# Neighbourhood attention on tiles of two half blocks: 64 queries with keys of their own, scores in plain fp32

## The chip, the cores and the metric

The kernel runs on one core of a Trainium2 chip. The metric is the device time of one launch in microseconds, the median of several runs. A program's engines are called PE (TensorE), DVE (VectorE), ACT (ScalarE), POOL (GpSimd) and SP (the queue that issues all transfers).

## What is computed

One encoder layer on two sequences, a prompt of 256 and a sample of 2048 tokens, both seen as a grid of 64 columns (4 and 32 rows). Half of the mixing is attention over a window of 8 rows by 16 columns around each query, with a bias by relative place; the other half is a Fourier mixing.

```python
def one_row(r):
    rs = jnp.clip(r - kr // 2, 0, rows - kr)          # kr = min(8, rows)
    k_slab = lax.dynamic_slice_in_dim(kg, rs, kr, axis=1)[:, :, slab_cols]
    v_slab = lax.dynamic_slice_in_dim(vg, rs, kr, axis=1)[:, :, slab_cols]
    logits = jnp.einsum('bjqhd,bijkhd->bhjqik', q_blk, k_slab).astype(jnp.float32) * scale
    logits = jnp.where(valid[:, :, None, :], logits + bias, NEG_INF)
    p = jax.nn.softmax(...)
    out = jnp.einsum('bhjqik,bijkhd->bjqhd', p, v_slab)

h = rms_norm(x, g_pre)
q, k, v, z_a, u_f, z_f = jnp.split(h @ w_in, ...)
mixed = concat([rms_norm(attention(q, k, v)) * silu(z_a), rms_norm(fourier(u_f)) * silu(z_f)])
out = x + rms_norm(mixed @ w_out, g_post)
```

There are 8 heads of 64 features; they are worked on in 4 pairs, one head on partitions 0 to 63 and the other on 64 to 127.

## The kernel before, in words

The program has three parts. First the projections (about 0 to 560 us): large matmuls in which each fp32 operand is split into a high and a low fp32r half, three products for one (`mm3`, L164 to L166). In this part the tables of the attention bias are also masked and written to DRAM (`t_load`, `t_mask`, `t_store`, L578 to L600). Then the Fourier part (to about 625 us), then attention together with the first half of the output projection (to 887 us), then the rest of the output projection.

Attention goes over 36 groups, `G`: for each head pair one group of the prompt (`R` is None) and eight of the sample (`R` 0 to 3 is a block of 8 query rows, `hc` the left or right half of the columns). A group has two query tiles `b` of 128 queries. In the sample a tile is 8 rows by 16 columns. All 128 queries share one rectangle of keys, which covers the windows of all of them: 11, 15, 15 or 12 rows (`NR`, from row `K0` on) by 24 or 32 columns (`KW`), so 264 to 480 keys; in the prompt 4 rows by 40 columns. What a query may not see is masked by the bias table.

For one group: `scores` multiplies q (K = 64, one head) with the keys into four PSUM tiles, a tile for each `b` and head. q and K are split into fp32r halves first (`split_q`, L1137; `split_k`, L1069, a quarter of K at a time, in the groups 5 to 8 of the pair before), by a cast on ACT and a subtraction on POOL, and three matmuls are summed (L1157). The heads' matmuls use rows 0 to 63 and 64 to 127 of the array. `bias_max` on DVE adds the table and takes the extreme (L1179), `exps` on ACT takes the exponential with its sum (L1184), `soft` on POOL scales (L1191). `transp` (L1462) turns the weights in chunks of up to 128 keys on PE into `ptb` and copies them to `pt` (one head by ACT, one by DVE). `pv` multiplies them with V, plain fp32, the heads in two column tiles of the array (L1478), then DVE multiplies by z, ACT squares, POOL sums.

The order on PE, ACT, DVE, POOL and SP is written by hand in the loop over `k`: scores of group `k`; transposes of `b` = 0 of group `k - 1`; six matmuls of the output projection of the Fourier half (`f_mm`, `po`, L1408); transposes of `b` = 1; six more; `pv` of group `k - 1`. So at each moment the vector engines work on group `k` while PE finishes group `k - 1`. K of the next pair is loaded at `i` = 3, the bias tables at `i` = 0, 3 and 7, q three groups ahead (`prep`), V and z one group ahead of the scores (`prep_v`).

Of the kernel before, what the change touches and what calls it, by code (L numbers as in the profile page):

```python
# [29 lines left out]
NR = (11, 15, 15, 12)  # L30
K0 = (0, 4, 12, 20)
KW = (24, 32, 32, 24)
KC0 = (0, 8, 24, 40)
YB = 2
# [9 lines left out]
def constants():  # L44
# [59 lines left out]
    cm = np.zeros((128, 2, 40))  # L104
    cs_ = np.zeros((128, 80))
    rm = np.zeros((128, 48))
    for p in range(128):
        for b in range(2):
            ws = min(max(32 * b + p % 32 - 8, 0), 48)
            kc = 24 * b + np.arange(40)  # L110
            cm[p, b] = np.where((kc >= ws) & (kc < ws + 16), 0.0, BIG)
        i, qc = divmod(p, 16)
# [4 lines left out]
        for r0, j in ((max(i - 4, 0), np.arange(11)), (i, 11 + np.arange(15)), (min(i, 4), 26 + np.arange(12))):  # L117
            rm[p, j] = np.where((j - j[0] >= r0) & (j - j[0] < r0 + 8), 0.0, BIG)
    c["cmask"] = cm.reshape(128, 80)
# [5 lines left out]
def layout(inp):  # L125
# [15 lines left out]
    d = np.arange(40)[None, :] - np.arange(32)[:, None]  # L141
    cols = np.clip(np.stack([d, d - 8]) + 15, 0, 30)
    rows = np.arange(4)[None, :] - np.arange(4)[:, None] + 7
    a["tp"] = rpb[:, rows[:, None, None, :, None], cols[None, :, :, None, :]].reshape(4, 2, 4, 2, 32, 4, 40) \
        .transpose(0, 2, 4, 3, 1, 5, 6).reshape(4, 128, 640)
    d = np.arange(32)[None, :] - np.arange(16)[:, None]
    cols = np.clip(np.concatenate([d[:, :24], d - 8, d[:, :24] - 8], 1) + 15, 0, 30)
    rows = np.clip(np.arange(15)[None, :] - np.arange(8)[:, None] + 3, 0, 14)
    a["tr"] = rpb[:, rows[:, None, :, None], cols[None, :, None, :]].reshape(8, 128, 1200)
# [19 lines left out]
def build(tc, A, O):  # L169
# [10 lines left out]
    vP = dr.tile([2, 4, 40, 512], F32, name="vP")  # L180
# [10 lines left out]
    tD = [dr.tile([4, 128, 2, 80 * n], F32, name="tD%d" % n) for n in (11, 15, 12)]  # L191
# [13 lines left out]
    cm = cst.tile([128, 2, 40], F32, name="cm")  # L205
# [130 lines left out]
    def vu_out(m, c):  # L336
        s, b = PL[c]
        o = st.tile([128, 512], F32, tag="f", name=m + "o", bufs=3)
        x = row_tile(c)
        nc.scalar.activation(o, acc.pop((m, c)), AF.Copy, scale=invt[:, x:x + 1])  # L340
        if s is not None:
            put_rows(m, 0, b, s, o)
        elif m == "u":
            nc.sync.dma_start(uD[c * 128:c * 128 + 128, :], o)
        else:
            for r in range(4):
                nc.sync.dma_start(vP[c, r, 8 * c:8 * c + 32], o[32 * r:32 * r + 32])
                x = 24 * (1 - c)
                nc.sync.dma_start(vP[1 - c, r, 32 * c:32 * c + 8], o[32 * r + x:32 * r + x + 8])
# [228 lines left out]
    def t_load(x):  # L578
        mt.extend(k8(F32, "mt", (128, 2048)) for y in range(2))
        nc.sync.dma_start(mt[0][:, :1200], A["tr"][x])  # L580

    def t_mask(x, q):
        rows = lambda a: a.rearrange("p (i x) -> p i x", x=80)
        base, out = rows(mt[0][:, :1200]), rows(mt[1][:, :1840])
        if q == 0:
            nc.vector.tensor_tensor(out=base, in0=csm.unsqueeze(1).to_broadcast([128, 15, 80]), in1=base,  # L586
                                    op=ALU.subtract)
            return
        o, i, m0, n = ((out[:, :11], base[:, 4:], 0, 11), (out[:, 11:], base[:, :12], 26, 12), (base, base, 11, 15))[q - 1]
        nc.gpsimd.tensor_tensor(out=o, in0=i, in1=rmask[:, m0:m0 + n].unsqueeze(2).to_broadcast([128, n, 80]),  # L590
                                op=ALU.add)

    def t_store(x, q):
        pr, h = divmod(x, 2)
        if q == 0:
            nc.sync.dma_start(tD[0][pr][:, h], mt[1][:, :880])
            nc.sync.dma_start(tD[2][pr][:, h], mt[1][:, 880:1840])
        else:
            nc.sync.dma_start(tD[1][pr][:, h], mt[0][:, :1200])
            mt.clear()  # L600
# [138 lines left out]
    for b in range(16):  # L739
# [25 lines left out]
        if kind % 2:  # L765
            i, d = p, o
        else:
            i = p.rearrange("p (b r c) -> p b r c", b=2, c=32)
            d = o.rearrange("p (r b c) -> p b r c", b=2, c=32)
        nc.scalar.activation(d, i, AF.Silu if kind < 2 else AF.Copy)  # L770
# [8 lines left out]
    def t_step(x, j):  # L779
        if j == 0:  # L780
            t_load(x)
        for q in {3: (0, 1), 4: (2,), 5: (3,)}.get(j, ()):
            t_mask(x, q)
        if j > 4:
            t_store(x, j - 5)
# [30 lines left out]
    for i in range(16):  # L816
# [22 lines left out]
        def dst(f, b):  # L839
            if kind % 2 == 0:  # L840
                return o[f].rearrange("p (x b c) -> p b x c", b=2, c=32)[:, b]
            if kind == 1:
                return o[f].rearrange("p (a b j) -> p b a j", b=2, j=256)[:, b]
            return o[f].rearrange("p (y b x c) -> p y x b c", y=2, b=2, c=16)[:, b]

        def src(a):
            if kind % 2 == 0:
                return a.rearrange("p (x c) -> p x c", c=32)
            if kind == 1:
                return a.rearrange("p (a j) -> p a j", j=256)  # L850
# [207 lines left out]
    KQ = T // 4  # L1058
# [6 lines left out]
    def fetch_k(kk, pr, x):  # L1065
        ts = slice(x * (T // 2), (x + 1) * (T // 2))
        nc.sync.dma_start(kk[1][:, ts].bitcast(F32), kD[pr, :, ts])

    def split_k(kk, x):  # L1069
        ts = slice(x * KQ, (x + 1) * KQ)  # L1070
        nc.scalar.copy(kk[0][:, ts], kk[1][:, ts].bitcast(F32))
        nc.gpsimd.tensor_tensor(out=kk[1][:, ts], in0=kk[1][:, ts].bitcast(F32), in1=kk[0][:, ts].bitcast(F32),
                                op=ALU.subtract)


    TB = {}

    def load_t(pr, kind):
        t = TB[pr, kind] = tp.tile([128, 2400], F32, tag="tb", name="tb", bufs=2)
        if kind == 0:  # L1080
            nc.sync.dma_start(t[:, :640], A["tp"][pr])
            nc.sync.dma_start(t[:, 640:].rearrange("p (h x) -> p h x", h=2), tD[0][pr])
        else:
            n = 80 * (15, 12)[kind - 1]
            nc.sync.dma_start(t[:, :2 * n].rearrange("p (h x) -> p h x", h=2), tD[kind][pr])

    def mask_p(pr):
        v = TB[pr, 0][:, :640].rearrange("p (b x c) -> p b x c", b=2, c=40)
        nc.gpsimd.tensor_tensor(out=v, in0=cm.unsqueeze(2).to_broadcast([128, 2, 8, 40]), in1=v, op=ALU.subtract)
# [3 lines left out]
    def group(pr, i):  # L1093
        if i == 0:
            return dict(pr=pr, R=None, ts=slice(0, TP), k0=0, nr=4, t=[(24 * b, 40) for b in range(2)])
        R, hc = divmod(i - 1, 2)
        t0 = TP + 512 * R + 256 * hc
        return dict(pr=pr, R=R, hc=hc, ts=slice(t0, t0 + 256), k0=4 + K0[R], nr=NR[R],
                    t=[(KC0[2 * hc + b], KW[2 * hc + b]) for b in range(2)])

    def prep(g):
        pr, ts = g["pr"], g["ts"]
        g["qh"] = jl.tile([128, 256], F32R, tag="qh", name="qh", bufs=4)
        g["ql"] = jl.tile([128, 256], F32R, tag="ql", name="ql", bufs=4)
        if g["R"] is None:
            q = qD[pr, :, ts].rearrange("p (b x) -> p b x", b=2)
        else:
            sg, x = divmod(g["R"], 2)
            t0 = TP + 1024 * sg + 512 * g["hc"]
            q = qD[pr, :, t0:t0 + 512].rearrange("p (b x) -> p b x", b=2)[:, :, 128 * x:128 * x + 128]  # L1110
        nc.sync.dma_start(g["ql"].bitcast(F32).rearrange("p (b x) -> p b x", b=2), q)


    def prep_v(g):
        cs = slice(g["pr"] * 128, g["pr"] * 128 + 128)
        g["v"] = jl.tile([128, 7, 128], F32, tag="v", name="v", bufs=VB)
        g["ch"], j = [], 0
        for b, (c0, w) in enumerate(g["t"]):
            n = g["nr"] * w
            if g["R"] is None:  # L1120
                src = vP[b]
            else:
                src = vD[2 * g["hc"] + b][K0[g["R"]]:K0[g["R"]] + g["nr"]]
            src = src.rearrange("r c e -> (r c) e")
            m = -(-n // 128)
            z = -(-n // m)
            f = n // z
            nc.sync.dma_start(g["v"][:z, j:j + f], src[:z * f, cs].rearrange("(j p) e -> p j e", p=z))
            if n % z:
                nc.sync.dma_start(g["v"][:n % z, j + f], src[z * f:, cs])  # L1130
            ch = [(z * x, min(z, n - z * x), j + x) for x in range(m)]
            g["ch"].append(ch)
            j += len(ch)
        g["za"] = jl.tile([128, 256], F32, tag="za", name="za", bufs=VB)
        nc.sync.dma_start(g["za"], zD[1, cs, g["ts"]])

    def split_q(g):  # L1137
        qh, ql = g["qh"], g["ql"]
        nc.scalar.copy(qh, ql.bitcast(F32))
        nc.gpsimd.tensor_tensor(out=ql, in0=ql.bitcast(F32), in1=qh.bitcast(F32), op=ALU.subtract)  # L1140


    def scores(g):
        nr = g["nr"]
        kk = [k.rearrange("p (r c) -> p r c", c=64) for k in KK[g["pr"]]]
        if "w" in g:
            sp = [ps.tile([128, 480], F32, tag="c", name="s", bufs=1), *ptb,
                  ps.tile([128, 480], F32, tag="a", name="s", bufs=3)]
# [590 lines left out]
```

## Time and profile before

| | us |
|---|---|
| median of 3 runs (994.31 to 996.14) | 996.02 |
| span of the profiled execution (first to last instruction) | 991.9 |
| TensorE busy | 976.3 |
| VectorE busy | 701.8 |
| ScalarE busy | 501.4 |
| GpSimd busy | 428.6 |

The profile is of one execution of its own; its span has no overhead of the launch in it. A row of the profile's groups gives line, engine, operation, written and read tiles, shape and count, then busy time, mean ns of one, and the idle time before it with what ended it. A row of the timeline begins with the start and the length in us, and like instructions that follow each other are one row. The weight loads of TensorE are an engine of their own (PEld), beside PE. In a matmul's shape `64*128 64x360` the first pair is the stationary operand, rows by columns, and the second the moving one.

### The profile page before, as it was taken

How to read it: one execution, taken by the hardware profiler on the slowest of the kernel's cores; microseconds unless marked ns; L12 is line 12 of the kernel's file. 1: busy time of each engine (PE TensorE's matmuls, PEld its weight loads, DVE VectorE, ACT ScalarE, POOL GpSimd, SP SyncE). 2: the span in 40 equal slices, each digit the busy share in tenths (PEclk: the TensorE clock that was granted, in tenths of full speed). 3: DMA queues.
4: the chain of work that ended last, by engine and by line, in shares of the span. 5: the costliest groups of instructions: out<-in, count | busy, mean ns of one | idle time of the engine just before them, and what ended most of it. 6: DMA issues, size and time to landing. Idle time of an engine off the chain costs nothing.

```text
span 991.9 us, 16973 instructions
## 1 busy us (share of the span) xinstructions
PE 976.3 (98%) x5774; PEld 806.4 (81%) x5774; DVE 701.8 (71%) x1301; ACT 501.4 (51%) x1083; POOL 428.6 (43%) x400
## 2 busy tenths in 40 slices
PE   7999999999999999999999999999999999999996
PEld 6889988888888888887788889878888888888885
DVE  5378987777866877686877354776656665658997
ACT  5846676423334633233343254676676666654443
POOL 3200002464741302565566023467577686534444
PEclk9999999999999999999999999999999999999998
DMA  8899586456847997499899798698778998979993
GB/s 315 308 378 342 189 323 249 171 205 250 300 169 301 361 411 252 180 328 325 308 325 331 272 322 308 205 287 272 249 212 267 261 314 270 285 245 337 345 338 127
DMA packets 145982, 278.70 MB, mean 281 GB/s; under 512 B 13096, under 2 KB 84072, under 8 KB 142504
## 3 DMA queue, kind: packets, MB, share of 16 engines
q1 hardware_dynamic: 145896, 277.62, 80.9%
q8 instruction: 46, 0.75, 0.3%
q14 instruction: 40, 0.33, 0.1%
HBM read 183.19 MB, written 101.71 MB: 287 GB/s over the span
## 4 chain that ended last, share of the span: by engine, by line
PE 92%; DVE 2%; ACT 2%; POOL 1%; issue 1%; DMA 1%; SPq 0%; DVEq 0%; POOLq 0%
PE po L1408 18%; PE mm L165 18%; PE mm L166 18%; PE mm L164 18%; PE ptb L1462 5%; PE pv L1478 5%; PE s L1157 4%; PE pab L1000 2%; ACT w L1184 1%; PE py L164 1%; PE py L166 1%; PE py L165 1%; DMA ut<-uN 1%; POOL w L1191 1%; POOL ql L1140 0%
## 5 line engine op out<-in xcount | busy, mean ns | idle before, releaser
L164 PE MATMUL mm<-xh,wa 128*128 128x512 f32 x448 | 176.9, 395 | 0.0
L166 PE MATMUL mm<-xh,wa 128*128 128x512 f32 x448 | 176.8, 395 | 0.0
L165 PE MATMUL mm<-xl,wa 128*128 128x512 f32 x448 | 176.8, 395 | 0.0
L537 POOL TENSOR_TENSOR ws<-wr 128x512 f32<-128x512 f32 x16 | 22.3, 1394 | 243.0 <-PE mm L165 128.3
L1191 POOL TENSOR_SCALAR w<-w,m 128x480 f32<-128x480 f32 (+6 forms) x136 | 81.4, 611 | 61.4 <-DVE m L1188 48.9
L165 PEld LDWEIGHTS mm<-xl,wa 128*128 128x128 f32 x448 | 84.4, 188 | 19.8
L166 PEld LDWEIGHTS mm<-xh,wa 128*128 128x128 f32 x448 | 84.4, 188 | 19.8
L164 PEld LDWEIGHTS mm<-xh,wa 128*128 128x128 f32 x448 | 84.4, 188 | 19.6
L1408 PE MATMUL po<-wo,yh 128*128 128x512 f32 x272 | 90.5, 414 | 0.0
L1184 ACT ACTIVATE w<-w,m 128x480 f32<-128x480 f32 (+6 forms) x136 | 79.3, 586 | 16.9 <-DVE m L1179 16.7
L1408 PE MATMUL po<-w,yh 128*128 128x512 f32 x280 | 86.7, 391 | 0.0
L552 DVE TENSOR_TENSOR wa<-wr,wa 128x512 fp32r<-128x512 f32 x60 | 60.5, 1014 | 31.9 <-ACT wa L551 31.9
L1179 DVE CUSTOM_DVE_ANT_1 w<-s,tb 128x360 f32<-128x360 f32 (+5 forms) x124 | 62.4, 541 | 9.6 <-PE s L1157 8.7
L590 POOL TENSOR_TENSOR mt<-mt,rmask 128x880 f32<-128x880 f32 (+2 forms) x24 | 53.4, 2239 | 30.3 <-DVE mt L586 17.0
L165 PE MATMUL mm<-vl,xh 128*128 128x512 f32 x168 | 66.1, 394 | 0.2 <-DVE vl L483 0.2
L164 PE MATMUL mm<-vh,xh 128*128 128x512 f32 x168 | 65.9, 392 | 0.0
L166 PE MATMUL mm<-vh,xl 128*128 128x512 f32 x168 | 65.9, 392 | 0.0
L854 DVE TENSOR_TENSOR f<-u,mm 128x512 f32<-128x512 f32 x64 | 43.6, 681 | 29.6 <-PE mm L166 24.7
L1408 PEld LDWEIGHTS po<-w,yh 128*128 128x128 f32 x280 | 52.3, 188 | 10.8 <-issue 0.2
L1462 PE MATMUL ptb<-ident,w 128*120 128x128 f32 (+5 forms) x428 | 59.7, 277 | 0.0
L551 ACT CAST wa<-wr 128x512 fp32r<-128x512 f32 x60 | 36.0, 616 | 45.8 <-PE mm L166 14.3
L1478 PEld LDWEIGHTS pv<-pt,v 120*64 120x64 f32 (+6 forms) x896 | 48.2, 136 | 12.9 <-issue 10.0
(253 smaller groups left out, 2406.8 us busy)
## 6 DMA issues: line engine op xcount, KB each, us to landing
wr<-wz SPq DMA_DIRECT2D x48, 512.0 KB
vl<-sD SPq DMA_DIRECT2D x20, 512.0 KB
xm<-xm SPq DMA_DIRECT2D x9, 1024.0 KB
oD<-ofs SPq DMA_DIRECT2D x18, 512.0 KB
of<-oD SPq DMA_DIRECT2D x18, 512.0 KB
yr<-yD SPq DMA_DIRECT2D x34, 256.0 KB
zD<-f SPq DMA_DIRECT2D x16, 512.0 KB
woD<-wo SPq DMA_DIRECT2D x16, 512.0 KB
```

The costliest lines, as they stand in the source:

```text
L164: nc.tensor.matmul(out, lh, rh, start=first, stop=False)
L165: nc.tensor.matmul(out, lh, rl, start=False, stop=False)
L166: nc.tensor.matmul(out, ll, rh, start=False, stop=last)
L552: nc.vector.tensor_tensor(out=o[:, 1], in0=src, in1=o[:, 0].bitcast(F32), op=ALU.subtract)
L590: nc.gpsimd.tensor_tensor(out=o, in0=i, in1=rmask[:, m0:m0 + n].unsqueeze(2).to_broadcast([128, n, 80]), op=ALU.add)
L854: nc.vector.tensor_tensor(out=dst(f, b), in0=src(uu[u]), in1=src(p), op=op)
L1179: nc.vector.tensor_tensor_reduce(out=rows(g["w"][b][:, h, :n], w), in0=rows(g["s"][2 * b + h][:, :n], w), in1=tv, scale=1.0, scalar=3.0e38 ...
L1184: nc.scalar.activation(w, w, AF.Exp, bias=m[:, h:h + 1], scale=-1.0, accum_out=m[:, 2 + h:3 + h])
L1191: nc.gpsimd.tensor_scalar(w, w, m[:, 4 + h:5 + h], 1.0, ALU.mult, ALU.mult)
L1408: nc.tensor.matmul(p, (d["l"] if x == 2 else d["h"])[:, c], w(n, int(x == 1), c), start=j == 0, stop=j == 11)
L1462: nc.tensor.transpose(ptb[h][:nk, j * 128:j * 128 + 128], g["w"][b][:, h, c0:c0 + nk], ident)
L1478: nc.tensor.matmul(p[hs, b], g["v"][:nk, v, hs], g["pt"][b][:nk, h, j * 128:j * 128 + 128], start=j == 0, stop=j == len(ch) - 1)
```

## The change

The 128 queries of a sample tile are now two halves of 4 rows by 16 columns, `HALF`: rows 0 to 3 with 28 to 31 (`R` 0), 4 to 11, 12 to 19, 20 to 27. A half has its own keys. At `R` 0 both halves lie at the grid's edge and see 8 rows each. At the others each half sees 11 rows, of which 7 are those of both; the second half's rows are taken in the order 7 to 10, 0 to 6 (`ORD`), so that the shared rows stand in the same place of the tile in both. In the prompt a half is a column block of 16 with 32 key columns.

- Scores: one plain fp32 matmul for each head and half (the second half at `R` > 0 in two pieces), in tiles of 64 rows by 64 columns of the array. Both splits, `split_q` and `split_k`, and the second copy of K are gone.
- Softmax works on 256, 192, 352, 264 or 128 keys a query.
- `transp` has chunks of four key rows: three for each `b` at `R` > 0 (the last of three rows), two at `R` 0, one in the prompt.
- `pv` has, at `R` > 0, two matmuls of 128 queries for the shared rows and one of 64 for each half's own; at `R` 0 and in the prompt all have 64 queries.
- V is loaded in two pieces for each `b` (in the prompt one for both), q and z in two pieces where the halves are not neighbours in DRAM; `R` 0 stores its result in two pieces.
- The bias tables: `t_mask` has one subtraction on DVE (19 rows by 80) and one addition on POOL (11 by 80) instead of one (15 by 80) and three; `tD` is one tensor, loaded in two parts per pair (`i` = 5 of the pair before and `i` = 0) instead of three. The prompt's table has 512 columns instead of 640, its V 4 x 4 x 32 rows instead of 2 x 4 x 40.
- The prompt's q is written in the order of halves (two ACT copies for one), the sample's z with its columns in order. The last output tiles go in the order 0 to 3, 16, 17, 4 to 15.

```diff
-NR = (11, 15, 15, 12)
-K0 = (0, 4, 12, 20)
+HALF = ((0, 28), (4, 8), (12, 16), (20, 24))
+ORD = ((0, 1, 2, 3, 4, 5, 6, 7, 8, 9, 10), (7, 8, 9, 10, 0, 1, 2, 3, 4, 5, 6))
...
     def load_k(pr):
-        kh = kp.tile([128, T], F32R, tag="kh", name="kh")
-        kl = kp.tile([128, T], F32R, tag="kl", name="kl")
-        return kh, kl
...
+        k = KK[pr] = kp.tile([128, T], F32, tag="kh", name="kk")
+        for x in range(2):
+            ts = slice(x * (T // 2), (x + 1) * (T // 2))
+            nc.sync.dma_start(k[:, ts], kD[pr, :, ts])
...
     def prep_v(g):
...
+            parts = ((0, 3, r0 - 4), (3, 1, r1 + 3)) if g["R"] else ((0, 2, 0), (2, 2, 24))
+            for j, m, r in parts:
+                nc.sync.dma_start(v[:n, 4 * b + j:4 * b + j + m],
+                                  src[r:r + 4 * m].rearrange("r c e -> (r c) e")[:, cs]
+                                  .rearrange("(j p) e -> p j e", p=n))
+            if g["R"]:
+                g["ch"].append([(0, n), (n, n), (2 * n, 3 * w)])
+                g["pp"].append([(1, None, n, 4 * b + 1, True, False), (2, None, 3 * w, 4 * b + 2, False, False),
+                                (0, 0, n, 4 * b, False, False), (0, 1, n, 4 * b + 3, False, True)])
...
-    def split_q(g):
-        qh, ql = g["qh"], g["ql"]
-        nc.scalar.copy(qh, ql.bitcast(F32))
-        nc.gpsimd.tensor_tensor(out=ql, in0=ql.bitcast(F32), in1=qh.bitcast(F32), op=ALU.subtract)
...
     def scores(g):
...
-        for b, (c0, w) in enumerate(g["t"]):
-            for x in range(3):
-                q = g["ql" if x == 2 else "qh"]
+        for b, w in enumerate(g["kw"]):
+            if R is None:
+                seq = [(y, 0, 4, 0, KP0[2 * b + y]) for y in range(2)]
+            else:
+                c0, r = KC0[2 * g["hc"] + b], 4 + HALF[R][0] - 4 * (R > 0)
+                seq = [(0, r, 11, 0, c0), (1, r + 11, 4, 0, c0), (1, r + 4, 7, 4, c0)] if R else \
+                    [(y, r + 24 * y, 8, 0, c0) for y in range(2)]
+            for y, k, n, j, c0 in seq:
                 for h in range(2):
                     hs = slice(64 * h, 64 * h + 64)
-                    nc.tensor.matmul(sp[2 * b + h][:, :nr * w], q[hs, 128 * b:128 * b + 128],
-                                     kk[x == 1][hs, g["k0"]:g["k0"] + nr, c0:c0 + w], start=x == 0, stop=x == 2)
+                    nc.tensor.matmul(sp[2 * b + h][64 * y:64 * y + 64, j * w:(j + n) * w],
+                                     g["q"][hs, 128 * b + 64 * y:128 * b + 64 * y + 64],
+                                     kk[hs, k:k + n, c0:c0 + w], start=True, stop=True)
...
     def pv(g):
...
-        for b, ch in enumerate(g["ch"]):
-            for j, (c0, nk, v) in enumerate(ch):
+        for b, pp in enumerate(g["pp"]):
+            for j, y, nk, v, first, last in pp:
+                o = slice(0, 128) if y is None else slice(64 * y, 64 * y + 64)
                 for h in range(2):
                     hs = slice(64 * h, 64 * h + 64)
-                    nc.tensor.matmul(p[hs, b], g["v"][:nk, v, hs], g["pt"][b][:nk, h, j * 128:j * 128 + 128],
-                                     start=j == 0, stop=j == len(ch) - 1)
+                    nc.tensor.matmul(p[hs, b, o], g["v"][:nk, v, hs], g["pt"][b][:nk, h, j * 128 + o.start:j * 128 + o.stop],
+                                     start=first, stop=last)
```

TensorE, from the scores of a group of the first pair to the transposes behind them, before (`s` scores, `ptb` transposes, `po` output projection; the size is that of what is written, partitions by columns):

```order
L1157 MATMUL s<-kh,qh 128x480 x2
L1157 MATMUL s<-kl,qh 128x480 x2
L1157 MATMUL s<-kh,ql 128x480 x2
L1157 MATMUL s<-kh,qh 128x360 x2
L1157 MATMUL s<-kl,qh 128x360 x2
L1157 MATMUL s<-kh,ql 128x360 x2
L1462 MATMUL ptb<-ident,w 120x128 x6
```

and the same place now:

```order
L1163 MATMUL s<-kk,q 64x352 x2
L1163 MATMUL s<-kk,q 64x128 x2
L1163 MATMUL s<-kk,q 64x224 x2
L1163 MATMUL s<-kk,q 64x264 x2
L1163 MATMUL s<-kk,q 64x96 x2
L1163 MATMUL s<-kk,q 64x168 x2
L1461 MATMUL ptb<-ident,w 96x128 x2
L1461 MATMUL ptb<-ident,w 72x128
L1461 MATMUL ptb<-ident,w 96x128 x2
L1461 MATMUL ptb<-ident,w 72x128
```

Twelve matmuls of 128 queries over 480 and 360 keys have become twelve of 64 queries over at most 352, without a sum over three.

TensorE, the end of an iteration, before (`pv` product with V of the group before):

```order
L1408 MATMUL po<-wo_5189,yh 128x512 x2
L1408 MATMUL po<-wo_5189,yl 128x512
L1478 MATMUL pv<-pt,v 64x128 x14
L1157 MATMUL s<-kh,qh 128x288 x2
L1157 MATMUL s<-kl,qh 128x288 x2
```

and now:

```order
L1407 MATMUL po<-wo_5143,yh 128x512 x2
L1407 MATMUL po<-wo_5143,yl 128x512
L1478 MATMUL pv<-pt,v 64x128 x4
L1478 MATMUL pv<-pt,v 64x64 x4
L1478 MATMUL pv<-pt,v 64x128 x4
L1478 MATMUL pv<-pt,v 64x64 x4
L1163 MATMUL s<-kk,q 64x128 x8
```

Fourteen matmuls of 128 queries have become eight of 128 and eight of 64.

SP, what is issued from the prompt's result `yD<-y` of the last pair on, before (`v<-vD` and `za` for the next group, `ql` for the one after that, `w` weights of the output projection, `yr` and `yz` the Fourier half):

```order
L1501 DMA yD<-y 128x256
L1128 DMA v<-vD_66 118x2x128
L1130 DMA v<-vD_66 116x128
L1128 DMA v<-vD_67 88x3x128
L1135 DMA za<-zD 128x256
L1111 DMA ql<-qD 128x2x128
L1549 DMA w_7937<-woD 128x1024
L1438 DMA oD<-ofs 128x1024
```

and now:

```order
L1512 DMA yD<-y 128x256
L1128 DMA v<-vD_66 128x2x128 x2
L1128 DMA v<-vD_67 96x2x128 x2
L1140 DMA za<-zD 128x128 x2
L1107 DMA q<-qD 128x2x128
L1556 DMA w_7828<-woD 128x1024
L1437 DMA oD<-ofs 128x1024
```

V comes in four transfers of 128 or 96 partitions instead of three of 118, 116 and 88, z in two; six issues between the result and `oD` have become eight.

More of the change, by code (lines that the diff above doesn't have):

```diff
@@ L1161, in scores @@
             return
[L1162 to L1163 removed]
+        wide = [w == 32 and (g["R"] is not None or b) for b, w in enumerate(g["kw"])]
+        g["w"] = [jp.tile([128, 2, 352 if x else 264], F32, tag="ww" if x else "wn", name="w", bufs=WB) for x in wide]
         g["m"] = [jp.tile([128, 8], F32, tag="m", name="m", bufs=4) for b in range(2)]
@@ L1213, in build @@
     prep(G[3])
-    for g in G[:2]:
-        split_q(g)
     pg = ExitStack()
@@ L1371, in build @@
     ftiles = [{"t": t, "half": 1} for t in range(18)]
-    atiles = [{"t": t, "half": 0, "i": t} for t in range(18)]
+    atiles = [{"t": t, "half": 0, "i": i} for i, t in enumerate((0, 1, 2, 3, 16, 17, *range(4, 16)))]
     def ys_load(d):
```

279 lines of the change are left out of this document (136 added, 143 removed).

## The prediction

> **What bounds the kernel now.** I read the page's totals and its chain first, then the busy time by stages, then the matmul timeline of single groups. The span is 991.9 us, the median of the three timed runs 996.02, so 4.1 us lie outside the span. The sum below is made against the span, and 4.1 is added at the end.
>
> ```profile
> PE 976.3 (98%) x5774; PEld 806.4 (81%) x5774; DVE 701.8 (71%) x1301; ACT 501.4 (51%) x1083; POOL 428.6 (43%) x400
> PE 92%; DVE 2%; ACT 2%; POOL 1%; issue 1%; DMA 1%; SPq 0%; DVEq 0%; POOLq 0%
> PE po L1408 18%; PE mm L165 18%; PE mm L166 18%; PE mm L164 18%; PE ptb L1462 5%; PE pv L1478 5%; PE s L1157 4%; PE pab L1000 2%; ACT w L1184 1%; PE py L164 1%; PE py L166 1%; PE py L165 1%; DMA ut<-uN 1%; POOL w L1191 1%; POOL ql L1140 0%
> ```
>
> TensorE is busy for 98% of the span and is 92% of the chain. Scores (`s`), transposes (`ptb`) and the product with V (`pv`) are 14% of it: about 139 us that the change can touch. The attention stage by stretches (columns: PE, PEld, DVE, ACT, POOL busy, then clock, DMA share, GB/s):
>
> ```profile
> 640.00:666.00 26.00, 25.67 (x228) 20.12 (x225) 20.58 (x56) 18.28 (x48) 16.89 (x19) 1.00 0.93 274
> 760.00:887.00 127.00, 127.00 (x1114) 103.99 (x1110) 77.15 (x252) 81.29 (x233) 81.55 (x114) 1.00 0.90 275
> ```
>
> No vector engine is above 80% of a stretch, the clock is full, and only the DMA share comes near PE. So the time goes with the length of TensorE's own pieces, and I price the change by them. A piece's length is its start to the next piece's start (the second column contains the drain of the last matmul). A group of key rows 4 to 18 or 12 to 26 (R 1 or 2, 15 key rows):
>
> ```profile
> 718.99 1.03 PE L1462 MATMUL ptb<-ident,w 128*120 128x128 f32 x8
> 719.78 0.70 PE L1408 MATMUL po<-wo,yh 128*128 128x512 f32 x2
> ...
> 721.35 1.75 PE L1478 MATMUL pv<-pt,v 120*64 120x128 f32 x28
> 723.02 0.44 PE L1157 MATMUL s<-kh,qh 64*128 64x360 f32 x2
> ...
> 723.46 0.33 PE L1157 MATMUL s<-kh,ql 64*128 64x360 f32 x2
> 723.63 0.38 PE L1157 MATMUL s<-kh,qh 64*128 64x480 f32 x2
> 723.85 0.38 PE L1157 MATMUL s<-kl,qh 64*128 64x480 f32 x2
> ...
> 724.38 1.09 PE L1462 MATMUL ptb<-ident,w 128*120 128x128 f32 x8
> ```
>
> Scores 1.36, `pv` 1.67, eight transposes 0.79. R 3 (12 key rows) has scores of 1.13, six transposes in 0.62, `pv` 1.46:
>
> ```profile
> 745.30 0.45 PE L1157 MATMUL s<-kh,qh 64*128 64x384 f32 x2
> ...
> 746.43 0.86 PE L1462 MATMUL ptb<-ident,w 128*96 128x128 f32 x6
> 747.05 0.71 PE L1408 MATMUL po<-wo,yh 128*128 128x512 f32 x2
> ...
> 750.65 1.53 PE L1478 MATMUL pv<-pt,v 96*64 96x128 f32 x24
> 752.11 0.34 PE L1157 MATMUL s<-kh,qh 64*128 64x160 f32 x2
> ```
>
> The prompt's group has four transposes in 0.39 and 0.36 and `pv` of 1.03; the scores at 700.69 are those of R 0, 1.05:
>
> ```profile
> 694.84 0.63 PE L1462 MATMUL ptb<-ident,w 128*80 128x128 f32 x4
> 695.23 0.71 PE L1408 MATMUL po<-wo,yh 128*128 128x512 f32 x2
> ...
> 697.74 0.61 PE L1462 MATMUL ptb<-ident,w 128*80 128x128 f32 x4
> 698.10 0.70 PE L1408 MATMUL po<-wo,yh 128*128 128x512 f32 x2
> ...
> 699.66 1.09 PE L1478 MATMUL pv<-pt,v 80*64 80x128 f32 x16
> 700.69 0.43 PE L1157 MATMUL s<-kh,qh 64*128 64x352 f32 x2
> ...
> 701.74 0.53 PE L1462 MATMUL ptb<-ident,w 128*88 128x128 f32 x3
> ```
>
> The prompt's scores take 0.84:
>
> ```profile
> 687.26 0.34 PE L1157 MATMUL s<-kh,qh 64*128 64x160 f32 x2
> ...
> 688.10 0.88 PE L1462 MATMUL ptb<-ident,w 128*128 128x128 f32 x6
> ```
>
> Three unit prices follow. A transpose: (0.79 - 0.36) / 4 = 0.11. A plain fp32 matmul stands as two records (14 matmuls of `pv` are 28); the two heads' column tiles run side by side, so 8, 12 and 14 pairs of records take 1.03, 1.46 and 1.67: 0.108 a step of 128 columns (0.84 ns a column), with 0.17 around them. A split-fp32r score step of 480 columns is 0.22 (723.63 to 723.85), 0.46 ns a column; three of it and three of 0.165 are 1.16, so 0.20 lie around the scores.
>
> **Transposes.** Fewer padded keys means fewer chunks: per head pair the prompt's group goes from 8 to 4, R 0 twice from 12 to 8, the four groups of R 1 and 2 from 14 to 12, R 3 stays at 12. That is 20 less per pair: 80 x 0.11 = **-8.8 us**, all on TensorE.
>
> **Product with V.** R > 0: per column tile 8 steps of 128 columns (keys that both halves share) and 8 of 64 (each half's own). R 0 has 16 and the prompt 8 steps of 64 and no other. No row has 64 columns with 64 columns of weights. The nearest, the last stage of the Fourier part, in three column tiles of 32:
>
> ```profile
> 583.07 0.72 PE L1000 MATMUL pab<-d,zg 128*32 128x64 f32 x24
> 583.62 0.68 PE L1000 MATMUL pup<-f,up 128*32 128x129 f32 x12
> 584.23 0.65 PE L1038 MATMUL ppq<-wf,cs 128*64 128x512 f32 x2
> ```
>
> 24 records of 64 columns, three at a time, are 8 steps in 0.55: 0.069 with the head. Half of 0.108 is 0.054. I take 0.065, nearer to the row, since the weights are twice as wide here. The upper bound is a full step, 0.108. R > 0 then takes 0.17 + 0.864 + 0.52 = 1.55 (-0.12 for R 1 and 2, +0.09 for R 3), R 0 1.21 (-0.25), the prompt 0.69 (-0.34). Per pair: -0.48 + 0.18 - 0.50 - 0.34 = -1.14; **-4.6 us** in all. The Trainium skill ("TensorE: Matmul & The Clock Gate", LDWEIGHTS) says that a weight load goes with its columns at 1.2 a ns, by which 64 columns would be 53 ns and the step the 0.054 of the low end; by it this term would be -8.5.
>
> **Scores.** Three fp32r passes over K = 64 in two row tiles become one plain fp32 matmul in four tiles of 64 by 64 (two heads, two halves). Per tile R > 0 streams 352 + 264 columns, R 0 256 + 192, the prompt twice 128, each twice. If the four tiles run side by side, that is 2 x 616 x 0.84 = 1.04, 0.75 and 0.43, and with 0.20 around them 1.24, 0.95 and 0.63. Against 1.36, 1.13, 1.05 and 0.84: -0.12 (R 1, 2), +0.11 (R 3), -0.10 (R 0), -0.21 (prompt); per pair -0.67, in all **-2.7 us**. No row of before shows four tiles in this shape. For it: two row tiles overlap in every `s` row, two column tiles in `pv`, and `pup` (129 columns, x12) shows three: its program order is two matmuls into the first tile, two into the second, two into the third, and all 12 records are through in 0.61 (583.62 to 584.23), near 4 steps with a switch; one after the other they would be 1.3.
>
> **The waits that go.** Splitting q and K into halves disappears from ScalarE and GpSimd:
>
> ```profile
> L1140 POOL TENSOR_TENSOR ql<-ql,qh 128x256 fp32r<-128x256 f32 x33 | 28.2, 855 | 0.0
> L1139 ACT CAST qh<-ql 128x256 fp32r<-128x256 f32 x32 | 13.0, 408 | 1.8 <-DMA ql<-qD 1.8
> L1072 POOL TENSOR_TENSOR kl<-kl,kh 128x576 fp32r<-128x576 f32 x12 | 17.1, 1422 | 0.0
> PEld s L1157 <- POOL ql L1140: 2.7, 7, 0.6
> ```
>
> Those engines are not the bound, so their 58 us are worth only what TensorE waited for: 2.7. What is late next at that place is the bank that VectorE frees, or q itself, which is loaded three groups ahead. I take **-2.0**, with bounds of 0 and -4 (GpSimd's queue also held the softmax scaling behind the K split). In the bias stage two of three mask adds on GpSimd go (24 to 8); TensorE waits for none of it, so 0. Shorter bias, exponential and copy instructions: 0, beside TensorE.
>
> **The queue and the transfers.** The one DMA queue takes about 64 issues per pair instead of 45 (V in two pieces per half of a group, q and z cut where rows are not adjacent). An issue:
>
> ```profile
> L1111 SPq DMA_DIRECT2D ql<-qD x36: 320/433/1922, 578.5 to 862.1; - x36
> tb<-tD SPq DMA_DIRECT2D x4, 1200.0 KB
> tb<-tD SPq DMA_DIRECT2D x4, 960.0 KB
> tb<-tD SPq DMA_DIRECT2D x4, 880.0 KB
> tb<-tp SPq DMA_DIRECT2D x4, 320.0 KB
> ```
>
> 19 more at 0.43 are 8 us of SP per pair of 65, behind which q, V and z of the next groups stand; they are asked for a group and more ahead, so I cost this at 0. Bytes fall: the bias tables from 3360 to 1776 KB per pair (256, 640 and 880), V rises by 1424 rows of 512 bytes, 712 KB.
>
> **Sum.** -8.8 - 4.6 - 2.7 - 2.0 = -18.1: span 973.8, time **978 us**.
>
> **Rivals.**
> - *Two tiles at a time.* If a tile's second record blocks those behind it in the queue, only the end of one matmul overlaps the start of the next. The scores' streams, (6 x 1.04 + 2 x 0.75 + 0.43) x 4 = 33 us, would double: 978 + 33 = 1011, slower. Against it is the `pup` row. It decides from 2.6 tiles at a time (18.1 = 33 x (4/c - 1)); three at a time would give 989. The Trainium skill states the rule behind it ("TensorE: Matmul & The Clock Gate", Part 3: Packing small matmuls): matmuls start and end strictly in program order. By that rule `pup` would be ten steps, 1.1 us; the trace disagrees.
> - *Half-width steps cost full ones.* If 64 columns take the 0.108 of 128 because the weights of each step are late, 88 half steps per pair cost 0.043 more: 15 us, 993. For it: with 128 columns of weights, 26 records of 64 columns take 3.12, 0.11 each:
>
> ```profile
> 573.14 3.12 PE L1000 MATMUL pab<-d,zg 128*128 128x64 f32 x26
> ```
>
>   Against it: the three-tile row, 0.069.
> - *Transfers take over.* The stretch 760 to 887 would shrink by its share, 127/265 of 18.1, to 118.3 us, with 0.90 x 127 = 114 us of DMA work in it, a share of 0.97. If V then lands late and the stretch can't go over the 0.93 of the busiest one, it takes 123: 982.5; at 0.90 nothing is gained there: 987. For it: more and smaller pieces; against it: fewer bytes.
>
> **How the numbers follow.** The main case has 0.79, two tiles 0.08, full half steps 0.05, transfers 0.08. Low end: half steps at 0.054 (-3.9) and waits at -4 (-2) give 972. High end: the transfers' 987 with half steps at 0.069 (+1.4), 988. That range leaves out the first two rivals, 0.13 together. A measurement tells about 0.2% (2 us) from no change: faster 0.90 (main, transfers, most of 993), same 0.03, slower 0.07.
>
> **What would show it.** Per group: scores of 1.24, 0.95, 0.63; `pv` of 1.55, 1.21, 0.69; transposes of 0.11; no wait of the scores for GpSimd. Scores near 2.3 would mean two tiles at a time; R 0's `pv` near 1.9, full half steps; matmuls of `pv` waiting for `v`, transfers. Wrong as a whole would be TensorE's pieces as forecast and the span unmoved.

## The result, and the profile after

| | before | after |
|---|---|---|
| median (runs), us | 995.16 (4: 993.62 to 996.14) | 972.75 (4: 972.25 to 973.30) |
| profiled execution, us | 993.62 | 973.30 |
| its span, us | 991.9 | 971.5 |

The ratio is 0.9779, with an interval of 0.9765 to 0.9793. The time fell by 22.4 us; 18.1 had been forecast. Between the two profiled executions it is 20.3 us, and 20.4 between their spans. In the later rounds, with 9 to 15 runs each, the kernel before had medians of 993.96 to 994.29, by which the fall is about 21.

The page of the changed kernel, its totals and its chain:

```profile
PE 956.3 (98%) x6222; PEld 791.3 (81%) x6222; DVE 670.6 (69%) x1305; ACT 468.8 (48%) x1036; POOL 334.6 (34%) x335
PE 96%; DMA 1%; DVE 1%; issue 0%; ACT 0%; DVEq 0%; SPq 0%; ACTq 0%
```

TensorE is busy for the same 98%, so the saving is in the length of its own work, and the chain is still TensorE's. The vector engines have lost 31 to 94 us each, of which little shows in the time (below). The end of the loop (PE, PEld, DVE, ACT, POOL, clock, DMA share, GB/s):

```profile
760.00:867.00 107.00, 105.53 (x1188) 86.69 (x1186) 60.05 (x215) 58.16 (x182) 52.69 (x82) 0.98 0.95 283
```

The loop ends 20 us earlier, at 867 instead of 887. In this stretch PE is idle for 1.5 us, the clock is below 1, and the DMA share has gone from 0.90 to 0.95. The matmul timeline of single groups, in which a piece's length is again its start to the next piece's start:

```profile
679.52 0.67 PE L1163 MATMUL s<-kk,q 64*64 64x128 f32 x16
680.12 0.88 PE L1461 MATMUL ptb<-ident,w 128*128 128x128 f32 x6
680.75 0.70 PE L1407 MATMUL po<-wo,yh 128*128 128x512 f32 x2
...
686.76 0.44 PE L1461 MATMUL ptb<-ident,w 128*128 128x128 f32 x2
686.96 0.71 PE L1407 MATMUL po<-wo,yh 128*128 128x512 f32 x2
...
691.20 0.69 PE L1478 MATMUL pv<-pt,v 128*64 128x64 f32 x16
691.82 0.99 PE L1163 MATMUL s<-kk,q 64*64 64x256 f32 x16
692.73 0.64 PE L1461 MATMUL ptb<-ident,w 128*96 128x128 f32 x4
693.13 0.70 PE L1407 MATMUL po<-wo,yh 128*128 128x512 f32 x2
...
703.64 1.15 PE L1478 MATMUL pv<-pt,v 128*64 128x64 f32 x32
704.73 1.28 PE L1163 MATMUL s<-kk,q 64*64 64x352 f32 x24
...
724.00 1.57 PE L1478 MATMUL pv<-pt,v 96*64 96x128 f32 x32
725.50 1.28 PE L1163 MATMUL s<-kk,q 64*64 64x264 f32 x24
726.71 0.87 PE L1461 MATMUL ptb<-ident,w 128*128 128x128 f32 x6
```

Scores take 0.60 in the prompt (679.52), 0.91 at R 0 (691.82) and 1.21 at R > 0 (725.50); 0.63, 0.95 and 1.24 had been forecast. `pv` takes 0.62 (691.20), 1.09 (703.64) and 1.50 (724.00), against 0.69, 1.21 and 1.55. Six transposes are 0.63, four 0.40, two 0.20.

One thing is new. TensorE's waits in the attention loop, and the place where both lie (pair 3, around the groups of R 0):

```profile
PE pv L1478 <- DMA v<-vD: 1.0, 1, 1.0
PE s L1163 <- DMA q<-qD: 0.5, 1, 0.5
```

```profile
811.43 0.71 PE L1407 MATMUL po<-wo,yh 128*128 128x512 f32 x2
...
814.02 1.50 PE L1478 MATMUL pv<-pt,v 96*64 96x64 f32 x32 [0.95 <-DMA v<-vD]
816.01 2.33 PE L1163 MATMUL s<-kk,q 64*64 64x264 f32 x24 [0.49 <-DMA q<-qD]
818.28 1.11 PE L1461 MATMUL ptb<-ident,w 128*128 128x128 f32 x4
819.04 0.87 PE L1407 MATMUL po<-wo,yh 128*128 128x512 f32 x2
```

```profile
816.00:819.00 3.00, 2.98 (x28) 2.35 (x29) 1.32 (x7) 0.99 (x3) 0.73 (x1) 0.50 1.08 332
```

TensorE is idle for 0.95 until V of this group lands, and for 0.49 until q of the scores behind it does. From the `po` at 811.43 to the scores at 816.01 stand 4.58 us where 1.55 and 1.09 would do: 1.9 lost. Behind it the granted clock is 0.50 (1.00 at 814 to 816, and again from 820 on), and scores of 2.27 and transposes of 0.76 stand where 1.21 and 0.40 would: 1.4 more, and 0.2 in the next `po`. Together 3.5 us, the only place of its kind. The 1.6 of the clock need not be in every execution: the mean clock of this one was 0.995, that of the three others 0.997 to 0.999. Why V is late there is read below.

### The profile page after: what moved, and what is told of

It reads as the page before. It is cut to its first block, busy times and chain, and to the rows that moved or that the text cites. A ratio compares the mean times of both kernels' runs of the same rounds, so it can differ in the third digit from the quotient of the medians.

```text
span 971.5 us, 17815 instructions
## 1 busy us (share of the span) xinstructions
PE 956.3 (98%) x6222; PEld 791.3 (81%) x6222; DVE 670.6 (69%) x1305; ACT 468.8 (48%) x1036; POOL 334.6 (34%) x335
## 4 chain that ended last, share of the span: by engine, by line
PE 96%; DMA 1%; DVE 1%; issue 0%; ACT 0%; DVEq 0%; SPq 0%; ACTq 0%
PE po L1407 20%; PE mm L174 18%; PE mm L175 18%; PE mm L173 18%; PE pv L1478 5%; PE ptb L1461 5%; PE s L1163 4%; PE pab L1005 2%; DMA oD<-ofs 1%; PE py L173 1%; PE py L175 1%; PE py L174 1%; PE pz L175 0%; PE ppq L1043 0%; PE pz L173 0%
## 5 line engine op out<-in xcount | busy, mean ns | idle before, releaser
L1197 POOL TENSOR_SCALAR w<-w,m 128x352 f32<-128x352 f32 (+4 forms) x136 | 77.4, 582 | 62.7 <-DVE m L1194 52.3
L562 DVE TENSOR_TENSOR wa<-wr,wa 128x512 fp32r<-128x512 f32 x60 | 57.0, 957 | 34.0 <-ACT wa L561 34.0
L1190 ACT ACTIVATE w<-w,m 128x352 f32<-128x352 f32 (+4 forms) x136 | 70.3, 519 | 13.6 <-DVE m L1185 13.4
L1185 DVE CUSTOM_DVE_ANT_1 w<-s,tb 128x264 f32<-128x264 f32 (+3 forms) x124 | 51.7, 454 | 11.7 <-PE s L1163 9.5
L1478 PEld LDWEIGHTS pv<-pt,v 96*64 96x64 f32 (+2 forms) x1088 | 44.8, 137 | 14.0 <-issue 9.6
L1407 PE MATMUL po<-w,yl 128*128 128x512 f32 x140 | 54.5, 390 | 0.0
L1407 PE MATMUL po<-wo,yl 128*128 128x512 f32 x136 | 53.5, 393 | 0.0
```

Source lines behind the costliest of these rows:

```text
L562: nc.vector.tensor_tensor(out=o[:, 1], in0=src, in1=o[:, 0].bitcast(F32), op=ALU.subtract)
L1185: nc.vector.tensor_tensor_reduce(out=rows(g["w"][b][:, h, :n], w), in0=rows(g["s"][2 * b + h][:, :n], w), in1=tv, scale=1.0, scalar=3.0e38 ...
L1190: nc.scalar.activation(w, w, AF.Exp, bias=m[:, h:h + 1], scale=-1.0, accum_out=m[:, 2 + h:3 + h])
L1197: nc.gpsimd.tensor_scalar(w, w, m[:, 4 + h:5 + h], 1.0, ALU.mult, ALU.mult)
L1407: nc.tensor.matmul(p, (d["l"] if x == 2 else d["h"])[:, c], w(n, int(x == 1), c), start=j == 0, stop=j == 11)
L1478: nc.tensor.matmul(p[hs, b, o], g["v"][:nk, v, hs], g["pt"][b][:nk, h, j * 128 + o.start:j * 128 + o.stop], start=first, stop=last)
```

## The experiments

The theory was the prediction's: TensorE's pieces set the time, four 64 x 64 tiles run side by side, and what other engines do is hidden. The rivals were that tiles run in program order, that the splits taken off ScalarE and GpSimd are what pays, and, after the result, that transfers hold part of the gain.

### Plain fp32 alone

The kernel before with its rectangles of keys, q and K plain fp32, no splits:

```diff
-            for x in range(3):
-                q = g["ql" if x == 2 else "qh"]
-                for h in range(2):
...
+            for h in range(2):
+                nc.tensor.matmul(sp[2 * b + h][:, :nr * w], g["ql"][hs, 128 * b:128 * b + 128],
+                                 kk[1][hs, g["k0"]:g["k0"] + nr, c0:c0 + w], start=True, stop=True)
```

> The kernel before with one thing of the change: scores in one plain fp32 matmul, no splits of q and K; tiles of 128 queries and their keys stay. My theory (the gain is fewer padded keys, 20 transposes and 1.8 us of V product per pair, and plain fp32 pays only because it runs in four tiles): two row tiles of plain fp32 cost 2 x 0.84 ns a column against 3 x 0.46, so 6256 columns per pair and 4 pairs give +7.1 us, less the 2.5 us that the scores waited beyond their length: about 1000, ratio 1.005, scores of 1.6 us for 15 key rows. Rival (freeing ScalarE and GpSimd of 58 us is what paid): 985 to 990, with the scores no longer than 1.36.

Measured: 998.25, ratio 1.0041 (1.0025 to 1.0057). The scores of a group of 15 key rows:

```profile
717.29 1.68 PE L1149 MATMUL s<-kl,ql 64*128 64x480 f32 x8
718.90 0.32 PE L1454 MATMUL ptb<-ident,w 128*120 128x128 f32 x1
```

They take 1.61, not the 1.36 of three fp32r passes: 2 x 840 columns x 0.84 + 0.20 is 1.61, the prediction's own price. The waits for GpSimd are gone here too, and the kernel is 4 us slower. So plain fp32 without the splits does not pay by itself. The rest of the change does, about 25 us: halves with keys of their own, and with them scores in four tiles, fewer transposes and shorter products with V.

### The order in which the tiles are fed

The changed kernel; the same score matmuls, all of one tile, then all of the next:

```diff
+        for y, h, b, w, k, n, j, c0 in sorted(todo, key=lambda a: a[:2]):
```

> The changed kernel with the score matmuls of a group issued tile by tile: all that one 64 by 64 tile has to do, then the next tile. Theory (each tile has its own order, the queue looks past a busy tile): scores stay at 1.21 us for 11 key rows, time 972 to 974. Rival (matmuls start in program order, neighbours in different tiles are what overlaps): a tile's matmuls stand one after the other, 3.3 us per group, about 70 us more, 1040; in between if the queue sees only a few instructions ahead.

Measured: 984.71, ratio 0.9897 (0.9881 to 0.9914), 12 us slower than the changed kernel. Two groups of R > 0:

```profile
701.08 1.79 PE L1166 MATMUL s<-kk,q 64*64 64x264 f32 x24
702.80 0.66 PE L1464 MATMUL ptb<-ident,w 128*128 128x128 f32 x4
```

```profile
708.73 1.94 PE L1166 MATMUL s<-kk,q 64*64 64x352 f32 x24
710.60 0.86 PE L1464 MATMUL ptb<-ident,w 128*96 128x128 f32 x6
```

The scores take 1.72 and 1.87, between the 1.21 of four tiles at a time and the 3.3 that I had estimated for one after the other. In the second group the first matmuls of three tiles start within 26 ns and that of the fourth 0.68 us after the first. So the queue does reach past a busy tile, but only some matmuls far: strict program order, the rule of the first rival, falls, and that order makes no difference falls too.

### Scores twice

Each score matmul issued twice into the same place:

```diff
+                    for again in range(2):
```

> The changed kernel with every score matmul issued twice into the same place. Theory (TensorE's own length passes to the end one for one): the streams of 1.01, 0.72 and 0.40 us per group, 6, 2 and 1 groups in each of 4 pairs, come again: +31.6 us, 1004. Rival (vector engines or transfers would have set the pace anyway, or the streams of the scores lie partly under waits): less than 20 us.

Measured: 1009.17, ratio 1.0146 (1.0131 to 1.0161): 36.4 us above the changed kernel.

```profile
703.43 1.81 PE L1164 MATMUL s<-kk,q 64*64 64x256 f32 x32
705.16 0.64 PE L1462 MATMUL ptb<-ident,w 128*96 128x128 f32 x4
...
710.02 2.54 PE L1164 MATMUL s<-kk,q 64*64 64x264 f32 x48
712.49 0.66 PE L1462 MATMUL ptb<-ident,w 128*128 128x128 f32 x4
```

R > 0 takes 2.47 instead of 1.21, R 0 1.73 instead of 0.91, the prompt 1.10 instead of 0.60. Per pair 7.6 + 1.6 + 0.5 = 9.7, in all 38.8, less the 3.5 of the wait for V with its clock, which this slower kernel does not have: 35.3. TensorE's time goes one for one into the end.

### The work taken off the vector engines, given back

Casts and subtractions of the splits' size, into unused tiles, at the places of the program where the splits stood:

```diff
+        nc.scalar.copy(h[:, :n], src)
+        nc.gpsimd.tensor_tensor(out=l[:, :n], in0=src, in1=h[:, :n].bitcast(F32), op=ALU.subtract)
```

> The changed kernel with the work of the splits given back to ScalarE and GpSimd, on scratch tiles that nobody reads: a copy and a subtraction of q in 35 groups, of a quarter of K in 12. Theory (these engines are not the bound; only the dependency of the scores on the split cost time): within 1 us of the changed kernel, 972 to 974. Rival (the engines' time is what the change bought): 3 us or more, 976 and above.

Measured: 974.16, ratio 0.9793 (0.9778 to 0.9807), 1.4 above: more than the theory's 1, less than the rival's 3, and the intervals of the two ratios overlap. The scores keep their 1.21; what grew is the wait for transfers:

```profile
PE s L1168 <- DMA q<-qD: 1.7, 2, 1.2
PE pv L1483 <- DMA v<-vD: 1.4, 1, 1.4
```

And the two mask additions of each table, given back to GpSimd in the projections:

```diff
+            for n in (12, 15):
+                nc.gpsimd.tensor_tensor(out=spare[:, :n], in0=t[:, :n],
+                                        in1=rmask[:, :n].unsqueeze(2).to_broadcast([128, n, 80]), op=ALU.add)
```

> The changed kernel with the two mask additions on GpSimd given back (12 by 80 and 15 by 80, into a spare tile that nobody reads), so GpSimd has 24 of them again. Theory (they ran beside TensorE, a wait of 0.8 us for the Fourier input at 447 us being all that could hang on them): 0 to 0.8 us more than the changed kernel, 972.5 to 973.5. Rival (the 1.1 us by which the projections end earlier, and more, are theirs): 974 and above.

Measured: 973.54 (972.15 to 975.06), ratio 0.9793 (0.9779 to 0.9806), 0.8 above, between theory and rival and inside the spread. The times do not decide, but the traces show a wait in the projections for the input of the Fourier part, here before and with the additions given back:

```profile
PE pz L165 <- DVE ut L373: 0.8, 1, 0.8
PE pz L174 <- DVE ut L383: 0.3, 1, 0.3
```

The two other kernels that have all the additions (the first experiment and the control below) show it with 0.6 and 0.5; the changed kernel and the nine others made from it do not show it. So the work of the splits is hidden but for a longer wait for transfers, and that of the mask is not quite hidden: it goes with a wait of 0.3 to 0.8.

### Moving the transfers

Three kernels moved one load each, and a fourth two of them, to have V in time. The output weights over twice as many iterations, from 14 on (and the same edit to the kernel before, as a control):

```diff
-        if 24 <= k < 32:
-            y = k - 24
+        if 14 <= k < 30 and k % 2 == 0:
+            y = (k - 14) // 2
```

> The changed kernel with the eight loads of the output weights (512 KB each) spread over iterations 14 to 28, one in two, instead of one in each of 24 to 31. Theory (the wait of about 3.5 us at 811 to 819, where the product with V waits for V and the scores for q at a DMA share of 1.0, comes from too many bytes in that stretch): the wait goes, 969 to 970. Rival (the wait comes from the number of issues on the one queue, 9 to 12 an iteration there, which stays about the same): 972 to 973, with the wait in the trace.

> The kernel before with the same spread of the output weights' loads. Theory (before, TensorE's own pieces were long enough to hide the transfers; its trace shows no wait of TensorE for one): no change, within 1 us of the kernel before. Rival (the stretch was held up by transfers before as well, without a wait that the profile names): 3 us less.

Measured: 974.06 (973.96 to 978.48), ratio 0.9808 (0.9790 to 0.9827); the control 994.17, 1.0002 (0.9993 to 1.0011). The control's time does not move. The changed kernel did not get faster, and in its profiled execution (its slowest, 978.48) TensorE waits five times for V and four for q. Then the second half of the bias table one iteration later, V one group earlier with a fourth buffer, and both:

```diff
-        if 0 < pr < 4 and i == 0:
+        if 0 < pr < 4 and i == 1:
```

```diff
-VB = 3
+VB = 4
...
-            prep_v(G[k + 1])
+            prep_v(G[k + 2])
```

> The changed kernel with the second bias table of a pair (880 KB) asked for one group later (i = 1), so that it no longer stands in the queue ahead of V and q of the pair's first sample groups. Theory (bunching: at i = 0 the table, a 512 KB piece of the output weights and 0.5 MB of Fourier tiles stand ahead of V): the wait at 811 to 819 shrinks by most of its 3.5 us, 969 to 971. Rival (the queue is behind over a longer stretch; what is moved away from here is late there): 972 to 974, waits elsewhere, as when the output weights were spread.

> The changed kernel with V and z asked for one group (7 us) earlier, into a fourth buffer. Theory (a late arrival by less than 2 us at one or two places): no wait for V is left, 969 to 970, whatever made it late. Rival (the transfers' rate itself is short over tens of us): the wait comes back later or at q, 972.

> The changed kernel with both, the table one group later and V and z one group earlier: the version that should beat both kernels. Theory: no wait of TensorE for a transfer, span 968, 969 to 970. Rival: V a group earlier only moves the wait to q or the table, 972.

Measured: 976.12, ratio 0.9814 (0.9801 to 0.9828); 977.03, 0.9830 (0.9815 to 0.9845); 978.22, 0.9845 (0.9824 to 0.9865). All slower than the changed kernel, against the theory in each. With the table later TensorE waits four times for V, 4.0 in all. With V earlier it never waits for V, and waits for q instead:

```profile
PE s L1163 <- DMA q<-qD: 5.3, 4, 2.5
```

Last, V on a queue of its own, ScalarE's:

```diff
-                nc.sync.dma_start(v[:n, 4 * b + j:4 * b + j + m],
+                nc.scalar.dma_start(v[:n, 4 * b + j:4 * b + j + m],
```

> The changed kernel with V's loads issued by ScalarE's queue instead of SP's: SP then has 5 to 6 issues an iteration instead of 9 to 10, the bytes stay. Theory (bytes in one stretch at a DMA share of 1.0): the wait stays, 972 to 974, ScalarE's 32 times 4 issues hidden. Rival (SP's issuing, 75% of the time at 0.5 us each, is what makes V late): the wait goes, 969 to 970.

Measured: 1015.96, ratio 1.0217 (1.0191 to 1.0243). ScalarE's timeline shows four issues that take 4.31 us and the exponential that stands behind them; TensorE then waits for its copies of `pt`, no longer for V or q, so theory and rival both fail:

```profile
640.96 4.31 ACTq L1128 DMA_DIRECT2D v<-vD  x4
645.32 0.52 ACT L1190 ACTIVATE w<-w,m 128x264 f32<-128x264 f32 x1 [3.98 <-DMA v<-vD]
```

```profile
PE ptb L1461 <- ACT pt L1463: 35.7, 27, 6.0
```

Two of these four issues begin within 0.02 us behind the landing of the transfer that last used their semaphore (642.03 and 644.90).

Why an issue comes so late is seen on SP in the changed kernel, in its timeline ahead of the late V, and in what SP waited for from 740 to 822 us (total, times, longest):

```profile
802.89 0.53 SPq L1079 DMA_DIRECT2D tb<-tD  x1
803.46 0.60 SPq L1556 DMA_DIRECT2D w<-woD  x1
804.17 0.37 SPq L1437 DMA_DIRECT2D oD<-ofs  x1
805.22 0.32 SPq L1512 DMA_DIRECT2D yD<-y  x1
806.08 3.28 SPq L1128 DMA_DIRECT2D v<-vD  x4
810.12 1.90 SPq L1140 DMA_DIRECT2D za<-zD  x2
812.95 0.37 SPq L1107 DMA_DIRECT2D q<-qD  x1
```

```profile
SPq L1107 <- DMA oD<-ofs: 2.3, 3, 0.9
SPq L1140 <- DMA tb<-tD: 2.1, 3, 1.1
SPq L1140 <- DMA w<-woD: 1.2, 1, 1.2
```

The transfers carry eight semaphores in turn, and an issue waits until the transfer eight places before it, the last owner of its semaphore, has landed. The first `za` at 810.12 is the eighth issue behind `tb`, which landed at 810.10; the second, at 811.68, stands eight behind `w` (landed 811.67), and `q` at 812.95 eight behind `oD` (812.93). So SP, which runs the program's order, is late by the landing of 640 and 512 KB pieces, and q, asked for three groups ahead in the program, is issued 3 us before it is used. V, issued from 806.08 on, lands behind the same 1920 KB (`tb`, `w`, `oD`, `yD`) between 813.89 and 815.03, when `pv` has stood since 813. Counted over 640 to 740 us, 4 of 97 issues before and 31 of 142 after begin within 0.15 us behind the landing of the transfer eight places back; in the kernel with scores twice, which does not wait, 6 of 126. The count differs between executions: in the last kernel below, whose program is the changed one's in this stretch, it is 15 of 140.

The last run leaves most bytes of one large load out and keeps every issue: of each piece of the output weights only 128 of 1024 columns.

```diff
-            nc.sync.dma_start(WO[y % 2][:, y // 2].bitcast(F32), woD[0, y % 2, y // 2])
+            nc.sync.dma_start(WO[y % 2][:, y // 2, :128].bitcast(F32), woD[0, y % 2, y // 2, :, :128])
+            nc.gpsimd.memset(WO[y % 2][:, y // 2, 128:].bitcast(F32), 0.0)
```

> The changed kernel with most of the output weights left out: of each of the eight pieces that are loaded in iterations 24 to 31 only the first 128 of 1024 columns come from DRAM (64 KB instead of 512), GpSimd writes zeros into the rest. Count and order of the issues stay. The loads are eight of the issues between 787 and 830 us; in the changed kernel V and q are late at 814 to 816 us, with a DMA share of 1.01 from 790 to 822, of which these weights are about 0.19 (4 of some 6.3 pieces of 128 packets of 4096 bytes, which are 0.29 of the packets' time). Theory (it is the bytes: the transfers of this stretch are at their rate, and whatever stands last in the queue comes late): the share falls to about 0.85, no wait of TensorE for v or q is left, and the time falls by what the wait cost, 3.6: 972.75 to about 969, ratio to before near 0.974. Rival (it is the issues: their count and order on SP, whatever their size): v and q are still waited for between 800 and 825, and the time stays at 972 to 974, ratio 0.978 to 0.979. Second rival (GpSimd's eight fills of 896 columns come ahead of the softmax scaling there): TensorE waits for the scaled weights and the time does not fall either, but then the wait is one of the transposes for GpSimd.

Measured: 970.21 (969.96 to 970.78), ratio 0.9760 (0.9747 to 0.9773). The intervals of the ratios overlap; the times themselves do not. The stretch before, in the changed kernel, and here:

```profile
790.00:822.00 32.00, 32.00 (x293) 26.45 (x293) 18.77 (x62) 22.78 (x64) 27.59 (x36) 1.00 1.04 308
790.00:822.00 32.00, 30.52 (x319) 24.28 (x315) 17.33 (x70) 17.51 (x59) 17.84 (x29) 0.95 1.01 305
790.00:822.00 32.00, 31.40 (x364) 24.82 (x357) 18.57 (x74) 17.65 (x61) 23.32 (x36) 1.00 0.87 253
```

The DMA share falls from 1.01 to 0.87 and the clock stays at 1.00; V is waited for no more, q still for 0.5 at the same group:

```profile
812.37 1.45 PE L1478 MATMUL pv<-pt,v 96*64 96x64 f32 x32
814.28 1.28 PE L1163 MATMUL s<-kk,q 64*64 64x264 f32 x24 [0.46 <-DMA q<-qD]
```

From the first `po` of the loop to the end of the last `pv` it is 2.5 us shorter (240.0 against 242.4), of the 3.5. Of that, 0.8 is V's: `pv` begins 0.2 behind its place (the last matmul of `po` begins at 811.83) instead of 1.0. Another 1.6 is the stretch at half clock, which this execution does not have. From `pv` to the scores it is still 1.91 where 1.09 would do, 1.99 in the changed kernel. So the theory holds for V, whose lateness was mostly the bytes in front of it, and not for q, which stays as late behind SP's lag. How much of the 2.5 between the medians is the bytes' stays open, since half clock does not always follow such a stop: with the splits' work given back TensorE stopped for 1.40 and 1.23 there, and the clock stayed at 1.00. That eight transfers at a time are what sets SP's lag is read from the traces and not tried: no kernel with more semaphores was run.

## Why the prediction was right, and where its sizes were off

- **Transposes**, -8.8: right. Per pair the four groups of R 1 and 2 save 0.22 each, R 0 0.43 twice, the prompt 0.39: -8.5 in all.
- **Product with V**, -4.6: right mechanism, mis-sized. A half step takes (1.09 - 0.17) / 16 = 0.058, not the 0.065 that I set nearer to the three-tile row than to half of a full step. With 1.50, 1.09 and 0.62 the term is -7.0, the largest miss among the savings. The Trainium skill ("TensorE: Matmul & The Clock Gate", LDWEIGHTS), by whose column rate I had estimated the step at 0.054 and the term at -8.5, was nearer than I was; the trace lies between.
- **Scores**, -2.7: right, a little better. -0.15 at R 1 and 2, +0.08 at R 3, -0.14 twice and -0.24 make -0.96 a pair, -3.8. How the price divides is another matter: scores twice add 1.26 for the 1232 columns of R > 0, 1.02 ns a column, which leaves nothing around them, where I had 0.84 and 0.20.
- **Waits that go**, -2.0: the groups of before whose scores were longer than their kind (up to 1.83 for 1.36, seven of them by 0.12 or more) lose 2.5. In the first experiment, without the splits, every kind has one length.
- **Sum**: -8.5 - 7.0 - 3.8 - 2.5 is -21.8; the transfer wait gives back 3.5 (1.9 of stop, 1.6 of half clock): -18.3. The loop itself, from the first `po` to the tail, went from 261.1 (626.04 to 887.14) to 242.4 (624.51 to 866.94): -18.7. So that the loop comes near the forecast of 18.1 is luck, two errors that cancel: 3.7 too little saved, 3.5 of a wait that had been costed at nothing.
- **The rest**: the loop begins 1.5 earlier. No term had that. For the mask additions the prediction has "TensorE waits for none of it, so 0"; by the rows above they go with a wait of 0.3 to 0.8, which is part of it. The rest is not told apart from scatter: the last `mm` matmul begins at 567.73 before, at 568.00 with the additions given back, and anywhere from 565.76 to 567.48 in the changed kernel and the nine others made from it. The tail is 0.2 shorter.
- **4.1 us outside the span**: wrong. It set the span of one execution against the median of others; that execution's own time was 993.62, 1.7 above its span. With 1.7, 973.8 would have been 975.5.
- **Transfers take over**, a rival of 0.08: came true in part. The step that failed is "they are asked for a group and more ahead, so I cost this at 0": the program asks that early, SP does not issue that early. The rival's place was right, its price (4.5 to 9 us) too high; its rule, a ceiling on the DMA share, does not hold either, since the stretch went to 0.95 and before had 1.04 from 790 to 822 without a wait. By the landings read above, what counts is which transfer stands behind which.
- **Two tiles at a time**, 0.08: refuted by 1.21, and in the order that would have shown it by 1.72 to 1.87. The Trainium skill's rule ("TensorE: Matmul & The Clock Gate", Part 3: Packing small matmuls), strict program order, would have made that order 3.3 by my estimate; the trace disagrees.
- **Half steps at full cost**, 0.05: refuted by 1.09 at R 0, where it needs 1.9.

## What to carry to other kernels

Where one engine is busy for 98%, price a change by the start-to-start lengths of its pieces, from the nearest rows, and take the time outside the span from the profiled execution itself. A load cut in more pieces costs places in the queue as well as issue time: read on SP whether an issue waits for a landing, and then what "asked for three groups ahead" means in microseconds; once the queue is short, moving one load forward only makes another one late. Feed small tiles of the array in turn, not one tile at a time.

## What the runs showed of the hardware

- The matmul queue reaches past a busy tile, but not without limit: 12 matmuls over four tiles take 1.21 us in turn and 1.72 to 1.87 tile by tile, where the first matmul of the fourth tile started 0.68 behind that of the first.
- A short stop of TensorE can cost more than itself: 1.9 us lost at 812 to 816 were followed by a granted clock of 0.50 from 816.0 to 819.4 and 1.6 us more. With V on ScalarE's queue each of the four stops of 2.79 to 5.95 us was followed by 0.50, for 3.4 or 6.8 us, and none of the shorter ones, up to 1.78, was. Between them length alone does not decide: with both moves a stop of 2.44 us was followed by 0.50 for 3.4, and with V one group earlier one of 2.45 by a clock of 1.00 and a piece of the usual length, 1.21:

```profile
819.72 1.28 PE L1163 MATMUL s<-kk,q 64*64 64x264 f32 x24 [2.45 <-DMA q<-qD]
820.93 0.66 PE L1461 MATMUL ptb<-ident,w 128*128 128x128 f32 x4
```

- A transfer issued on ScalarE's queue holds ScalarE while it waits for its semaphore: four issues, 4.31 us. Four that did not wait took 2.07 (at 652.11), so the issues alone are not free either.
